# Two of the weight sums of each Strassen pair move from VectorE to GpSimd

## The chip, the cores and the metric

The kernel runs on one core of one Trainium2 chip. The time is the device time of that core in microseconds (us), as the median of several runs. The span in the profile is the time from the first to the last instruction of one profiled execution.

## The reference

Two layers, each a feed-forward block (FFN), a token mixer and a second FFN, on 512 tokens of width 1024, all in float32. The change lies in the FFN, of which there are four in the run:

```python
def swiglu(x, w_in, w_out):
    gate, up = jnp.split(x @ w_in, 2, axis=-1)
    return (jax.nn.silu(gate) * up) @ w_out

# per layer: x is 512 x 1024, D_FF = 2816
hn = rms_norm(h, g_ffn1[l]) * (1.0 + sc1) + sh1
h = h + 0.5 * (1.0 + gt1) * swiglu(hn, w_ffn1_in[l], w_ffn1_out[l])
```

## The kernel before

Activations are held transposed, with the 1024 features in 8 tiles of 128 partitions and the 512 tokens along the free dimension. Every float32 product is made of three matmuls in a reduced format: weights and activations are split into a high part (a rounded copy) and a low part (the rest), and the products high by high, high by low and low by high are added up in PSUM. `split` (L100 to L102) makes the two parts of a tile: a cast on ScalarE (L101) and a subtraction on VectorE (L102).

The hidden width of 2816 is 22 blocks of 128, taken two at a time as 11 pairs, in two groups: pairs 0 to 5 and pairs 6 to 10. After each group comes a stage that multiplies the group's activations by the output weights and adds the result to the residual (L294). The first pairs of an FFN (four in the first FFN, two in the others) are computed in the plain way. All others, 34 over the run, go through `pair_in` (L388 to L429), which computes gate and up of two blocks with a scheme of Strassen's kind. The input width is halved, the tokens are halved, and seven products of a half weight by a half activation take the place of eight. A group's first Strassen pair is called the first pair of a stage in what follows; there are eight such starts.

The weights of a pair are four tiles of 128 by 1024 elements: A(0,0), A(0,1), A(1,0), A(1,1) (512 KB each). `raw` loads one by a DMA that SyncE issues; `plus` adds another one on top of it by an accumulating DMA that GpSimd issues (L334). The tile `S` (named `sum` in the profile, with two buffers sum0 and sum1 used by even and odd pairs) takes three values in turn, and each is split and multiplied:

- the first sum, A(1,0) + A(1,1), made by the two DMAs: product with P1 into `pF`;
- the second sum, with a11 = A(0,0) added (L403): product with P2 into `pD`;
- the third sum, with a12 = A(0,1) added (L413): product with B22 into `pF`.

The other four products are a11 by B11 into `pD`, a12 by B21 into `pG`, S3 = A(0,0) + A(1,0) (two DMAs again, tile `third`) by T3 into `pD`, and A(1,1) by T4 into `pD`. The last one belongs to `rest`, which is put off until the next pair calls `flush`. Since `pD` accumulates over four of the products, it has to be copied out in between: ScalarE copies it after a11's product (L402, tile s1) and after the second sum's product (L407, s2), and the next product onto `pD` waits for that copy. VectorE combines the results (L411, L417, L419, L421, L426) and splits the activations (L386).

Each of the tags wH and wL has four buffers, so splits run up to four products ahead of TensorE; the next cast then waits until TensorE gives a buffer back. Each engine runs its own instructions in order. That order, and the semaphores between the engines, are laid down by the framework when the program is built, from the order of the code, its dependences and its own estimate of when each instruction is ready. So the order in the profile isn't that of the code line by line: in the first pair of a stage, for one, a12's product begins before the second sum's.

GpSimd carries only the issue of DMAs (the accumulating loads, and those of the modulation weights `wada`, L177) and a few fills. The modulation weights are multiplied on VectorE (L163) in the output stages.

## Time and profile before

| | |
|---|---|
| median of 3 runs | 1936.84 us (1936.34 to 1939.99) |
| the profiled execution, its own time | 1942.73 us |
| its span | 1940.6 us |
| TensorE matmuls busy | 1894.4 us (98%) |
| VectorE (DVE) busy | 1400.0 us (72%) |
| ScalarE (ACT) busy | 838.4 us (43%) |
| GpSimd (POOL) busy | 130.8 us (7%) |
| mean granted TensorE clock | 0.990 |

In the views, PE is TensorE, DVE VectorE, ACT ScalarE, POOL GpSimd and SP SyncE. A row of the timeline gives the start in us from the span's start, the duration in us, the engine, the line, the operation, output and inputs by the program's names, and in brackets the idle time of the engine just before it with what ended it. A row of the waits gives who waited for whom: us in total, times, longest. Group rows give the count, the least, median and greatest duration in ns, and the first and last start. Matmuls are pipelined, so their starts say more than their durations.

### The profile page before, as it was taken

How to read it: one execution, taken by the hardware profiler on the slowest of the kernel's cores; microseconds unless marked ns; L12 is line 12 of the kernel's file. 1: busy time of each engine (PE TensorE's matmuls, PEld its weight loads, DVE VectorE, ACT ScalarE, POOL GpSimd, SP SyncE). 2: the span in 40 equal slices, each digit the busy share in tenths (PEclk: the TensorE clock that was granted, in tenths of full speed). 3: DMA queues.
4: the chain of work that ended last, by engine and by line, in shares of the span. 5: the costliest groups of instructions: out<-in, count | busy, mean ns of one | idle time of the engine just before them, and what ended most of it. 6: DMA issues, size and time to landing. Idle time of an engine off the chain costs nothing. (4 is left out here: it accounts for less than half of the span.)

```text
span 1940.6 us, 36814 instructions
## 1 busy us (share of the span) xinstructions
PE 1894.4 (98%) x15392; PEld 1748.4 (90%) x15392; DVE 1400.0 (72%) x2176; ACT 838.4 (43%) x1269; POOL 130.8 (7%) x212
## 2 busy tenths in 40 slices
PE   8999999999999999999999999999999999999999
PEld 7998899797889999899899989988978899998997
DVE  7687687658975787677877776876588578773762
ACT  4443255347422554155345514544562235532551
POOL 0101101000000000110100020010000000010100
PEclk8999999999999999999999999999999999999999
DMA  7767875621222475886746688773222125765742
GB/s 296 250 161 232 258 197 170 211 69 47 54 60 63 133 203 168 279 216 173 227 123 180 171 263 234 184 221 97 88 54 57 51 61 153 205 218 131 197 113 90
DMA packets 104325, 308.44 MB, mean 159 GB/s; under 512 B 23392, under 2 KB 24416, under 8 KB 103136
## 3 DMA queue, kind: packets, MB, share of 16 engines
q1 hardware_dynamic: 75936, 203.34, 32.5%
q0 software_dynamic: 28224, 102.77, 21.5%
q8 instruction: 120, 1.97, 0.4%
q14 instruction: 45, 0.37, 0.1%
HBM read 302.66 MB, written 3.41 MB: 158 GB/s over the span
## 5 line engine op out<-in xcount | busy, mean ns | idle before, releaser
L101 ACT CAST wH<-wraw 128x1024 fp32r<-128x1024 f32 (+2 forms) x292 | 268.9, 922 | 561.7 <-PE ps_mm L91 157.5
L102 DVE TENSOR_TENSOR wL<-wraw,wH 128x1024 fp32r<-128x1024 f32 (+2 forms) x292 | 309.0, 1060 | 123.3 <-ACT wH L101 121.8
L91 PE MATMUL ps_mm<-actL,wH 128*128 128x512 f32 (+1 forms) x744 | 282.5, 380 | 0.0
L90 PE MATMUL ps_mm<-actH,wH 128*128 128x512 f32 (+1 forms) x744 | 282.5, 380 | 0.0
L92 PE MATMUL ps_mm<-actH,wL 128*128 128x512 f32 (+1 forms) x744 | 282.0, 379 | 0.0
L380 PE MATMUL ps_d<-comH,wH 128*128 128x256 f32 x816 | 227.6, 279 | 4.5 <-ACT s L402 3.8
L381 PE MATMUL ps_d<-comL,wH 128*128 128x256 f32 x816 | 226.2, 277 | 0.0
L382 PE MATMUL ps_d<-comH,wL 128*128 128x256 f32 x816 | 226.1, 277 | 0.0
L98 PE MATMUL ps_mm<-hnH,wH 128*128 128x256 f32 x1040 | 213.8, 287 | 5.3 <-ACT hnH L101 2.9
L98 PE MATMUL ps_mm<-hnH,wL 128*128 128x256 f32 x1040 | 213.9, 285 | 0.5 <-DVE wL L102 0.5
L98 PE MATMUL ps_mm<-hnL,wH 128*128 128x256 f32 x1040 | 212.5, 284 | 0.0
L163 DVE SCALAR_TENSOR_TENSOR wada<-wada,crep 128x1024 f32<-128x1024 f32 x140 | 167.8, 1221 | 53.8 <-DMA wada<-in_wadaT 53.6
L102 DVE TENSOR_TENSOR wL<-sum,wH 128x1024 fp32r<-128x1024 f32 x102 | 125.0, 1225 | 70.1 <-ACT wH L101 69.9
L98 PEld LDWEIGHTS ps_mm<-hnH,wH 128*128 128x128 f32 x1040 | 160.8, 191 | 13.6 <-issue 5.5
L101 ACT CAST wH<-sum 128x1024 fp32r<-128x1024 f32 x102 | 107.5, 1054 | 148.0 <-PE ps_d L381 72.1
L98 PEld LDWEIGHTS ps_mm<-hnH,wL 128*128 128x128 f32 x1040 | 161.2, 191 | 6.3 <-issue 4.7
L98 PEld LDWEIGHTS ps_mm<-hnL,wH 128*128 128x128 f32 x1040 | 161.6, 191 | 4.5 <-issue 3.9
L92 PEld LDWEIGHTS ps_mm<-actH,wL 128*128 128x128 f32 x744 | 141.2, 190 | 26.1
L91 PEld LDWEIGHTS ps_mm<-actL,wH 128*128 128x128 f32 x744 | 141.2, 190 | 25.6
L90 PEld LDWEIGHTS ps_mm<-actH,wH 128*128 128x128 f32 x744 | 140.9, 189 | 25.7
L380 PEld LDWEIGHTS ps_d<-comH,wH 128*128 128x128 f32 x816 | 153.9, 189 | 7.1 <-ACT s L402 5.0
L381 PEld LDWEIGHTS ps_d<-comL,wH 128*128 128x128 f32 x816 | 154.1, 189 | 0.0
(401 smaller groups left out, 4245.5 us busy)
## 6 DMA issues: line engine op xcount, KB each, us to landing
wada<-in_wadaT POOLq DMA_DIRECT2D x128, 512.0 KB, 5.0
wraw<-in_wmi SPq DMA_DIRECT2D x40, 512.0 KB
wraw<-in_w2p SPq DMA_DIRECT2D x36, 512.0 KB
wraw<-in_w1p SPq DMA_DIRECT2D x32, 512.0 KB
wraw<-in_w1o SPq DMA_DIRECT2D x32, 384.0 KB
wraw<-in_w2o SPq DMA_DIRECT2D x32, 384.0 KB
wraw<-in_w1i SPq DMA_DIRECT2D x20, 512.0 KB
wraw<-in_w1o SPq DMA_DIRECT2D x32, 320.0 KB
```

What stands on the lines that cost most here:

```text
L90: mm(acc, wH, xH, start=start, stop=False)
L91: mm(acc, wH, xL, start=False, stop=False)
L92: mm(acc, wL, xH, start=False, stop=stop)
L98: mm(acc[:, sl], w[a][:, k], x[b][:, sl], start=start and n == 0 and sl is HALVES[0], stop=stop and n == 2, skip_group_check=True)
L101: nc.scalar.copy(hi, src)
L102: nc.vector.tensor_sub(lo, src, hi.bitcast(F32))
L163: stt(w, w, 1.0, crep, ALU.mult, ALU.mult, accum_out=out_)
L380: mm(pt[:, i], wH, x[k][0], start=start and i + k == 0, stop=False, skip_group_check=True)
L381: mm(pt[:, i], wH, x[k][1], start=False, stop=False, skip_group_check=True)
L382: mm(pt[:, i], wL, x[k][0], start=False, stop=k == 3, skip_group_check=True)
```

## The change

The two additions of weights on the tile `S` are issued on GpSimd in place of VectorE, with the same operands. `tt` is `nc.vector.tensor_tensor`.

```diff
                 prod(pD, hl(a11), B11, True)
                 s1 = half_("s1")
                 nc.scalar.copy(s1, pD)
-                tt(S, S, a11, ALU.add)
+                nc.gpsimd.tensor_tensor(S, S, a11, ALU.add)
                 flush()
                 prod(pD, hl(S), P2, False)
...
                 gate = half_("gate")
                 tt(gate, pG, s1, ALU.add)
                 act(gate, gate, AF.Silu)
-                tt(S, S, a12, ALU.add)
+                nc.gpsimd.tensor_tensor(S, S, a12, ALU.add)
                 S3 = raw(A(0, 0), "third")
                 plus(S3, A(1, 0))
```

## The prediction

> **What bounds the kernel now.** I read the busy table first, then a window over one pair in the middle of a Strassen stage, then the timelines of that pair, and last the list of what TensorE waits for. The window is one pair long (the seven products of `pair_in`).

> ```profile
> core 0: us, PE busy (x) PEld busy (x) DVE busy (x) ACT busy (x) POOL busy (x), PEclk, DMA share, GB/s
> 255.70:274.80 19.10, 19.10 (x170) 19.10 (x169) 15.24 (x16) 11.04 (x15) 1.70 (x2) 1.00 0.76 193
> ```

> TensorE is busy for all 19.10 us, VectorE for 15.24, GpSimd for 1.70. So in the middle of a stage an instruction taken from VectorE returns nothing by itself; what counts is whether the sums still come in time. The group rows of the tile `sum` give the two additions, 34 times each:

> ```profile
> L403 DVE TENSOR_TENSOR sum<-sum,first x34: 1216/1225/1227, 120.1 to 1854.3; 128x1024 f32<-128x1024 f32 x34
> L413 DVE TENSOR_TENSOR sum<-sum,wraw x34: 1215/1218/1226, 123.8 to 1863.0; 128x1024 f32<-128x1024 f32 x34
> ```

> Each takes 1.22 us, 83 us of VectorE time in all. Here they stand in that pair on VectorE (start and duration in us first), each behind the low-part split (L102) that reads the same tile:

> ```profile
> 256.56 1.23 DVE L102 TENSOR_TENSOR wL<-sum,wH 128x1024 fp32r<-128x1024 f32 x1 [0.89 <-ACT wH L101]
> 257.82 1.23 DVE L403 TENSOR_TENSOR sum<-sum,first 128x1024 f32<-128x1024 f32 x1
> ...
> 264.72 1.23 DVE L102 TENSOR_TENSOR wL<-sum,wH 128x1024 fp32r<-128x1024 f32 x1 [0.28 <-ACT wH L101]
> ...
> 266.47 1.22 DVE L413 TENSOR_TENSOR sum<-sum,wraw 128x1024 f32<-128x1024 f32 x1
> ```

> And here is who reads the results on ScalarE:

> ```profile
> 263.63 1.06 ACT L101 CAST wH<-sum 128x1024 fp32r<-128x1024 f32 x1 [1.66 <-PE ps_f L381]
> ...
> 271.83 1.06 ACT L101 CAST wH<-sum 128x1024 fp32r<-128x1024 f32 x1 [1.14 <-PE ps_d L381]
> ...
> 275.51 0.58 ACT L407 COPY s<-ps_d 128x512 f32<-128x512 f32 x1
> ```

> The casts do not wait for the sums. They wait for TensorE to give a weight buffer back. The second sum is ready at 259.05 (257.82 + 1.23) and read at 263.63, so it has 4.58 us to spare; the third is ready at 267.69 and read at 271.83, 4.14 us to spare. The splits have slack too. The matmul group rows of L380 place three products (first and last start behind the durations):

> ```profile
> L380 PE MATMUL ps_f<-hnH,wH x8: 276/276/276, 260.8 to 263.2; 128*128 128x256 f32 x8
> L380 PE MATMUL ps_f<-comH,wH x8: 276/276/276, 263.5 to 265.9; 128*128 128x256 f32 x8
> L380 PE MATMUL ps_d<-hnH,wH x8: 276/278/283, 266.3 to 268.7; 128*128 128x256 f32 x8
> ```

> One product takes 2.7 us (260.8 to 263.5 to 266.3). The split begun at 256.56 ends at 257.79 and feeds the product at 263.5: 5.7 us to spare.

> What is left to gain or lose lies where TensorE does wait, at the first pair of a stage. Of the list of TensorE's waits, two rows touch these lines:

> ```profile
> PE ps_g L382 <- DVE wL L102: 6.1, 5, 1.5
> ...
> PE ps_d L380 <- ACT s L402: 3.8, 3, 1.8
> ```

> Together 9.9 us in 8 waits. That is the ceiling of a gain from this change: 0.5%.

> **The change, part by part.** It removes 34 + 34 additions from VectorE and adds them to GpSimd, with the same operands and the same readers. No transfer is added. What moves is GpSimd's queue: it issues the accumulating loads of `plus`, and in order, so an addition that waits for its operands holds what is queued behind it.

> *Price of an addition on GpSimd.* The trace has no arithmetic on this engine. Its nearest row is a fill:

> ```profile
> L930 POOL MEMSET Sc<- 128x512 f32 x4 | 2.0, 531 | 57.9 <-DVE hn_t L246 57.9
> ```

> That is 0.53 us for 512 elements per partition, 1.06 us for one pass over 1024. An addition reads two tensors and writes one. Lower end: all three overlap as on VectorE, about 1.2 us. Upper end: three passes, 3.2 us. I take two passes, 2.1 us, the middle. [...]

> *Does VectorE go on beside it?* No row shows the two engines reading SBUF together. One end: both run freely. Other end: one after another, a VectorE instruction with two SBUF operands (all splits) waiting until the addition is over. I work out both.

> *Middle of a stage: nothing, in both cases.* The second sum could start at 257.8 and would end at 259.9 (at 261.0 with 3.2 us), before 263.63. The third could start at 265.95, where the split ends, or at 266.5, where it starts now, and would end by 268.6 (269.7), before 271.83. One after another VectorE would be held for at most 15.24 - 2.4 + 4.2 = 17.0 us of 19.1, and its splits have over 5 us to spare. What hides the edit is TensorE's own product time; an addition of over 5.3 us (266.5 to 271.83) would end that.

> *First pair of a stage: here it costs.* Three stage starts (near 690, 830 and 1180 us) have the third sum ahead of the split of a12. The one near 830, on VectorE:

> ```profile
> 830.39 1.23 DVE L403 TENSOR_TENSOR sum<-sum,first 128x1024 f32<-128x1024 f32 x1 [2.97 <-DMA first<-in_w2p]
> 831.54 1.22 DVE L102 TENSOR_TENSOR wL<-first,wH 128x1024 fp32r<-128x1024 f32 x1
> 832.81 1.23 DVE L102 TENSOR_TENSOR wL<-sum,wH 128x1024 fp32r<-128x1024 f32 x1
> 834.07 1.23 DVE L413 TENSOR_TENSOR sum<-sum,wraw 128x1024 f32<-128x1024 f32 x1
> ...
> 835.88 1.22 DVE L102 TENSOR_TENSOR wL<-wraw,wH 128x1024 fp32r<-128x1024 f32 x1
> ```

> On ScalarE:

> ```profile
> 831.73 1.05 ACT L101 CAST wH<-sum 128x1024 fp32r<-128x1024 f32 x1 [0.28 <-DVE sum L403]
> 832.69 1.05 ACT L101 CAST wH<-wraw 128x1024 fp32r<-128x1024 f32 x1
> ...
> 835.88 1.05 ACT L101 CAST wH<-sum 128x1024 fp32r<-128x1024 f32 x1
> 836.83 0.58 ACT L402 COPY s<-ps_d 128x512 f32<-128x512 f32 x1
> ```

> And on TensorE:

> ```profile
> 837.15 0.38 PE L382 MATMUL ps_g<-hnH,wL 128*128 128x256 f32 x1 [1.01 <-DVE wL L102]
> ...
> 838.55 0.28 PE L380 MATMUL ps_d<-comH,wH 128*128 128x256 f32 x1
> ```

> The first thing to see: the copy L402 stands behind the cast of the third sum in ScalarE's queue, and the product at 838.55 writes onto what L402 copies. So a late third sum delays that product. One after another: second sum 830.4 to 832.5; cast of it 832.6 to 833.65; split of a11 832.5 to 833.7, split of the sum to 834.95, split of a12 right behind to 836.1 (1.0 before its old end of 837.1, so the wait of 1.01 goes); third sum 836.1 to 838.2; its cast from 838.3, L402 from 839.25 to 839.85; product at about 839.9. That is 1.35 us later than 838.55. Freely, the third sum runs 835.05 to 837.15, L402 ends at 838.8: 0.3 later. With 3.2 us one after another, both sums add 1.1: 3.55 later. With 1.2 us: 0.5 earlier. Near 1180 the rows have the same order and distances:

> ```profile
> 1180.45 1.23 DVE L403 TENSOR_TENSOR sum<-sum,first 128x1024 f32<-128x1024 f32 x1 [5.47 <-DMA first<-in_w1p]
> ...
> 1184.14 1.22 DVE L413 TENSOR_TENSOR sum<-sum,wraw 128x1024 f32<-128x1024 f32 x1
> ```

> I give the start near 690 the same price; its third sum is the first row here. Two starts (near 1040 and 1647 us) have the third sum behind the split of a12:

> ```profile
> 690.74 1.22 DVE L413 TENSOR_TENSOR sum<-sum,wraw 128x1024 f32<-128x1024 f32 x1
> ...
> 1036.67 1.23 DVE L102 TENSOR_TENSOR wL<-sum,wH 128x1024 fp32r<-128x1024 f32 x1 [1.13 <-ACT wH L101]
> ...
> 1038.41 1.22 DVE L102 TENSOR_TENSOR wL<-wraw,wH 128x1024 fp32r<-128x1024 f32 x1
> ...
> 1040.15 1.22 DVE L413 TENSOR_TENSOR sum<-sum,wraw 128x1024 f32<-128x1024 f32 x1
> ...
> 1647.25 1.22 DVE L413 TENSOR_TENSOR sum<-sum,wraw 128x1024 f32<-128x1024 f32 x1
> ```

> TensorE near 1043, at the first product that needs the copy L402:

> ```profile
> 1043.04 0.39 PE L380 MATMUL ps_d<-comH,wH 128*128 128x256 f32 x1 [1.79 <-ACT s L402]
> ```

> GpSimd can begin the third sum at 1037.95 and end it at 1040.05, 1.3 before 1041.37: freely, about 0.9 of the 1.79 goes. One after another the split of a12 is held until 1040.05 and ends at 1041.25 in place of 1039.63, so a12's product loses 1.6, which is nearly what the later wait gives back. I take +0.25 on average over the two, between -0.9 (freely) and +1.35 (3.2 us). The other three starts show no wait for VectorE, and I cost them at nothing.

> **The sum**, one after another with 2.1 us: 3 x 1.35 + 2 x 0.25 = **+4.6 us**. Freely: 3 x 0.3 - 2 x 0.9 = -0.9. At 3.2 us one after another: 3 x 3.55 + 2 x 1.35 = +13.4. At 1.2 us: 3 x -0.5 - 2 x 0.9 = -3.3. Three of these four corners give a later or an equal time, so I take +4.6. The profiled execution took 1942.73 us (span 1940.6), so its like would take 1947.3; on the median of the runs shown, 1936.84, that is **1941.4 us**.

> **The rivals.**

> 1. *Freely, no stall* (20%): -0.9 us, 1935.9. The sums are longer but off the path, and VectorE does not notice. For it: VectorE idles for 3.9 of 19.1 us in the window. Against: the order on ScalarE, where L402 sits behind the cast.
> 2. *The other side, faster* (15%): VectorE loses two additions just where TensorE waits for its splits, so the 6.1 us row goes, and as the third sum starts earlier part of the 3.8 us row: -5 to -9.9, some 1930. It decides if an addition takes under about 1.5 us with no hold on VectorE, or if the copy L402 comes ahead of the cast in the new order.
> 3. *GpSimd's queue* (10%): the accumulating load of the next pair's first sum goes out between the two additions now:

> ```profile
> 259.27 0.85 POOL L334 DMA_DIRECT2D sum<-in_w1p  x1 [1.74 <-DVE sum L403]
> ...
> DMA to landing us min/median/max: 5.2/7.0/9.6
> ```

> In the code it stands behind the third sum. If it is queued so, it goes out at 268.6 and lands at 275.6 at the median, up to 278.2; its cast (1.05 us), and behind it L407 with 0.58, would end at 277.2 to 279.8. The product which needs L407 is the one ahead of 260.8, at 258.1, and a pair later at 258.1 + 19.1 = 277.2. So nothing to 2.6 us in each of some 26 pairs; with 1 us it is +26, 1963.

> [...]

> **How the numbers follow.** Forecast 55%: +1 to +13 us, of which 36 points lie above 3.9 us. I call over 0.2% (3.9 us) a difference, about what a measurement of this kernel can tell from none. Slower: 0.36 + 0.10 = 0.46. Same: 0.19 of the forecast and rival 1, 0.39. Faster: rival 2, 0.15. The range 1930 to 1954 takes in rival 2's middle and 3.2 us one after another (1950.2), with some room for other starts; it leaves out rival 3 and the tails, under 0.2.

> **What would show it.** Right: L403 and L413 on POOL at about 2.1 us; splits beside them at over 2 us or behind idle time that ends with `POOL sum`; TensorE's list with more for `ps_d L380 <- ACT s L402` and less for `ps_g L382`; the window of a pair still 19.1 us. Wrong: an addition of over 5 us, TensorE waits in the middle of a stage, a late accumulating load in POOL's rows, or a new order on ScalarE. The working assumes that the order on each engine stays as it is; a new one moves each start by up to a few us either way.

## The result, and the profile after

| | before | after |
|---|---|---|
| median (10 runs each, same chip) | 1936.81 us (1933.26 to 1940.78) | 1944.31 us (1938.34 to 1951.3) |
| the profiled execution, its own time | 1942.73 us | 1943.92 us |
| its span | 1940.6 us | 1942.2 us |

The ratio is 1.0043, with a 95% interval of 1.0027 to 1.0058: slower by 0.43%, about 8 us. Measured once more on another occasion, as a control for the experiments, the ratio was 1.0029 (1.0009 to 1.0049), about 6 us. The two profiled executions differ by only 1.6 us in span. That isn't the effect: the ten executions of before spread over 7.5 us and those of after over 13, for which the last section gives the likely reason, and the profiled execution of before is slower than all ten in the table. So totals are compared by medians here, and profiles only stage by stage; a difference from this profile of before comes out rather too small.

The busy table of after:

```profile
PE 1894.8 (98%) x15392; PEld 1749.3 (90%) x15392; DVE 1426.2 (73%) x2108; ACT 837.9 (43%) x1269; POOL 307.8 (16%) x280
```

The first thing to see is VectorE. It gave away 68 additions, 83 us, and its busy time rose, from 1400.0 to 1426.2 us. The group rows say how. First the two additions on GpSimd (count, least, median and greatest ns):

```profile
L403 POOL TENSOR_TENSOR sum<-sum,first x34: 2387/2694/3259, 120.3 to 1856.1; 128x1024 f32<-128x1024 f32 x34
L413 POOL TENSOR_TENSOR sum<-sum,wraw x34: 2386/2777/2802, 125.2 to 1864.1; 128x1024 f32<-128x1024 f32 x34
```

Then the splits of the raw weights on VectorE, from the groups of instructions (busy us, mean ns, idle before), in before:

```profile
L102 DVE TENSOR_TENSOR wL<-wraw,wH 128x1024 fp32r<-128x1024 f32 (+2 forms) x292 | 309.0, 1060 | 123.3 <-ACT wH L101 121.8
L102 DVE TENSOR_TENSOR wL<-first,wH 128x1024 fp32r<-128x1024 f32 x34 | 41.4, 1216 | 0.1
```

and in after:

```profile
L102 DVE TENSOR_TENSOR wL<-wraw,wH 128x1024 fp32r<-128x1024 f32 (+2 forms) x292 | 366.3, 1256 | 140.7 <-ACT wH L101 139.1
L102 DVE TENSOR_TENSOR wL<-first,wH 128x1024 fp32r<-128x1024 f32 x34 | 90.9, 2674 | 16.8 <-ACT wH L101 16.7
```

The splits of a11 went from 1.22 to 2.67 us in the mean: in these two groups alone 57.3 + 49.5 = 107 us came back. The pair in the middle of a stage shows them beside the additions. VectorE in after:

```profile
259.07 4.10 DVE L102 TENSOR_TENSOR wL<-first,wH 128x1024 fp32r<-128x1024 f32 x1 [0.28 <-ACT wH L101]
...
267.28 3.32 DVE L102 TENSOR_TENSOR wL<-wraw,wH 128x1024 fp32r<-128x1024 f32 x1
```

GpSimd in after:

```profile
259.39 2.69 POOL L403 TENSOR_TENSOR sum<-sum,first 128x1024 f32<-128x1024 f32 x1
261.75 1.15 POOL L334 DMA_DIRECT2D sum<-in_w1p  x1
266.73 2.77 POOL L413 TENSOR_TENSOR sum<-sum,wraw 128x1024 f32<-128x1024 f32 x1 [3.84 <-DVE wL L102]
```

A split of 1.22 us takes 4.10 beside one addition and 3.32 beside the other; each ends about 1.1 us after the addition does. Over the run 66 splits beside an addition are held like this. None of the 28 VectorE operations with an input in PSUM that overlap one is (near 690 us, L454 takes 0.68 beside L413). GpSimd is held as well: the third sums that begin while VectorE's L421 (two inputs in SBUF) is at work take 2.77 to 2.80 us, the others 2.39 to 2.42. The casts that read the sums have not moved:

```profile
263.48 1.05 ACT L101 CAST wH<-sum 128x1024 fp32r<-128x1024 f32 x1 [1.72 <-PE ps_f L381]
...
271.68 1.06 ACT L101 CAST wH<-sum 128x1024 fp32r<-128x1024 f32 x1 [1.19 <-PE ps_d L381]
```

And a window one pair long shows TensorE full and VectorE fuller (17.48 us in place of 15.24):

```profile
core 0: us, PE busy (x) PEld busy (x) DVE busy (x) ACT busy (x) POOL busy (x), PEclk, DMA share, GB/s
256.21:275.31 19.10, 19.10 (x171) 19.10 (x170) 17.48 (x14) 11.26 (x16) 6.88 (x4) 1.00 0.75 199
```

So the middle costs nothing. TensorE's products of the Strassen stages come in the same order in both kernels, so their starts can be subtracted one by one. This table does it for each stage, numbered by its first product's start in before: how much later the kernel is after the first two pairs than it was just ahead of the stage. (From the second pair's end to the stage's end the change is 0.00 us in all eight stages, in every kernel of this table.)

| stage start, us | 122 | 227 | 687 | 830 | 1032 | 1180 | 1640 | 1786 | sum |
|---|---|---|---|---|---|---|---|---|---|
| after | +0.45 | -0.72 | +3.35 | -0.42 | -1.63 | +0.93 | +0.64 | -0.03 | +2.6 |
| after, second profile | +0.73 | -0.72 | +3.41 | +1.21 | -0.55 | +2.35 | -1.19 | -0.04 | +5.2 |

One start is alike in both and stands out, that at 687. TensorE's waits in after name it:

```profile
PE ps_g L382 <- DVE wL L102: 6.8, 5, 1.8
...
PE ps_d L380 <- ACT s L407: 2.6, 1, 2.6
...
PE ps_d L382 <- DVE wL L102: 2.0, 2, 1.5
```

The row for L402 (3.8 us before) is gone. The row ps_d L382 is new: near 1044 and 1190 us the split of a11, held by the second sum, is late for its own product. The row for L407 is new too and is a single wait. Its chain, in before, on VectorE, SyncE's queue, GpSimd and ScalarE:

```profile
685.52 1.22 DVE L102 TENSOR_TENSOR comL<-q,comH 128x1024 fp32r<-128x1024 f32 x1
686.77 0.33 SPq L330 DMA_DIRECT2D sum<-in_w2p  x1
690.81 0.86 POOL L334 DMA_DIRECT2D sum<-in_w2p  x1 [20.91 <-DVE silu L454]
697.97 1.05 ACT L101 CAST wH<-sum 128x1024 fp32r<-128x1024 f32 x1 [3.63 <-PE ps_d L381]
```

The same instructions in after, with the addition ahead of them and the copy L407 and TensorE's product behind:

```profile
684.92 3.25 POOL L403 TENSOR_TENSOR sum<-sum,first 128x1024 f32<-128x1024 f32 x1 [12.97 <-DVE wL L102]
685.83 3.42 DVE L102 TENSOR_TENSOR comL<-q,comH 128x1024 fp32r<-128x1024 f32 x1
689.28 0.33 SPq L330 DMA_DIRECT2D sum<-in_w2p  x1
694.11 0.87 POOL L334 DMA_DIRECT2D sum<-in_w2p  x1 [1.10 <-DMA sum<-in_w2p]
701.50 1.04 ACT L101 CAST wH<-sum 128x1024 fp32r<-128x1024 f32 x1 [5.69 <-DMA sum<-in_w2p]
702.46 0.58 ACT L407 COPY s<-ps_d 128x512 f32<-128x512 f32 x1
703.09 0.39 PE L380 MATMUL ps_d<-comH,wH 128*128 128x256 f32 x1 [2.59 <-ACT s L407]
```

Read it downwards. The addition holds VectorE's last split of the combined activations (comL) from 1.22 to 3.42 us. That split reads tile `q`, which lies in the buffer sum1; only when it is over may SyncE load the next pair's sum into sum1, so the load goes out at 689.28 and not at 686.77. The accumulating load follows it, 3.3 us later than before. Before, the cast of that sum waited for TensorE; now it waits for the DMA, and the copy L407, which stands behind the cast in ScalarE's queue, makes TensorE wait 2.59 us.

### The profile page after: what moved, and what is told of

Its sections match the earlier page's. It is cut to its first block, busy times and chain, and to the rows that moved or that the text cites. A ratio compares the mean times of both kernels' runs of the same rounds, so it can differ in the third digit from the quotient of the medians.

```text
span 1942.2 us, 36888 instructions
## 1 busy us (share of the span) xinstructions
PE 1894.8 (98%) x15392; PEld 1749.3 (90%) x15392; DVE 1426.2 (73%) x2108; ACT 837.9 (43%) x1269; POOL 307.8 (16%) x280
## 3 DMA queue, kind: packets, MB, share of 16 engines
HBM read 302.66 MB, written 3.41 MB: 158 GB/s over the span
## 4 chain that ended last, share of the span: by engine, by line
PE 73%; DVE 11%; DMA 9%; ACT 4%; issue 3%; POOL 1%; SPq 0%; ACTq 0%; POOLq 0%; DVEq 0%
PE ps_mm L98 14%; PE ps_mm L91 7%; PE ps_mm L90 7%; PE ps_mm L92 7%; PE ps_d L380 6%; PE ps_d L381 6%; PE ps_d L382 6%; PE ps_f L382 3%; PE ps_f L380 3%; PE ps_f L381 3%; DVE wL L102 2%; DMA wada<-in_wadaT 2%; ACT wH L101 2%; PE ps_g L382 2%; DVE wada L163 1%
## 5 line engine op out<-in xcount | busy, mean ns | idle before, releaser
L101 ACT CAST wH<-wraw 128x1024 fp32r<-128x1024 f32 (+2 forms) x292 | 269.1, 922 | 564.2 <-PE ps_mm L91 160.9
L102 DVE TENSOR_TENSOR wL<-wraw,wH 128x1024 fp32r<-128x1024 f32 (+2 forms) x292 | 366.3, 1256 | 140.7 <-ACT wH L101 139.1
L380 PE MATMUL ps_d<-comH,wH 128*128 128x256 f32 x816 | 227.7, 279 | 3.2 <-ACT s L407 2.6
L381 PE MATMUL ps_d<-comL,wH 128*128 128x256 f32 x816 | 226.5, 278 | 0.0
L382 PE MATMUL ps_d<-comH,wL 128*128 128x256 f32 x816 | 226.5, 278 | 0.0
L101 ACT CAST wH<-sum 128x1024 fp32r<-128x1024 f32 x102 | 107.4, 1053 | 166.5 <-PE ps_d L381 75.0
L102 DVE TENSOR_TENSOR wL<-sum,wH 128x1024 fp32r<-128x1024 f32 x102 | 124.6, 1221 | 60.9 <-ACT wH L101 60.4
L380 PEld LDWEIGHTS ps_d<-comH,wH 128*128 128x128 f32 x816 | 154.3, 189 | 5.4 <-ACT s L407 4.5
L381 PEld LDWEIGHTS ps_d<-comL,wH 128*128 128x128 f32 x816 | 154.4, 189 | 0.0
```

The lines of the kernel that those rows point to most:

```text
L101: nc.scalar.copy(hi, src)
L102: nc.vector.tensor_sub(lo, src, hi.bitcast(F32))
L380: mm(pt[:, i], wH, x[k][0], start=start and i + k == 0, stop=False, skip_group_check=True)
L381: mm(pt[:, i], wH, x[k][1], start=False, stop=False, skip_group_check=True)
L382: mm(pt[:, i], wL, x[k][0], start=False, stop=k == 3, skip_group_check=True)
```

## The experiments

The ratios and intervals are those on record; they are not the quotients of the two medians beside them. The diffs leave out lines that only pass names along.

**Which pairs carry the cost.** Theory: the first pair of each stage alone. Rival: a small loss in every pair. In the first kernel, shown as a diff against after, the eight first pairs keep their sums on VectorE and the other 26 have them on GpSimd (`waiting` is empty in a first pair); the second is the other way round.

```diff
-                X = new_x(p)
+                X, sum_ = new_x(p), nc.gpsimd.tensor_tensor if waiting else tt
...
-                nc.gpsimd.tensor_tensor(S, S, a11, ALU.add)
+                sum_(S, S, a11, ALU.add)
...
-                nc.gpsimd.tensor_tensor(S, S, a12, ALU.add)
+                sum_(S, S, a12, ALU.add)
```

> The two sums stay on VectorE in the first pair of each stage (8 pairs) and go to GpSimd in the other 26. Theory (the cost lies at the first pairs, the middle of a stage is free although VectorE's splits are held there): the time of before, ratio 0.999 to 1.001, TensorE's waits as before. Rival A (held splits and a busier GpSimd queue cost in the middle): the +0.43% stays, 1.003 to 1.005. Rival B (the difference is clock drops that fall by chance): something between, 1.001 to 1.003.

Measured: 1938.28 us beside 1937.46 of before, ratio 0.9999 (0.9984 to 1.0014). The second kernel has `tt if waiting else nc.gpsimd.tensor_tensor`:

> The reverse: GpSimd makes the two sums in the first pair of each stage only (16 additions), VectorE makes the other 52. Theory: the whole cost, ratio 1.003 to 1.006 (+6 to +11 us). Rival A: the time of before, 0.999 to 1.001. Rival B: between.

Measured: 1941.21 us, ratio 1.0022 (1.0008 to 1.0035). Its waits, in the Strassen products:

```profile
PE ps_g L382 <- DVE wL L102: 5.7, 4, 1.8
...
PE ps_d L380 <- ACT s L407: 2.5, 2, 2.3
```

So 52 additions in the middle are free, and 16 at the first pairs cost. The cost is below the 1.003 that the theory expected, and in the range of rival B (clock drops that fall by chance). The record lists a mean granted clock for each execution, and here it is 0.9915 in the mean beside 0.9907 of before; 0.0008 of 1940 us is about 1.6 us, so by this estimate the 4.5 us that it costs in the mean would be about 6 at an equal clock. With the sums of the first pairs on GpSimd the L407 wait is there; the first of the two kernels has no such row.

**Which of the two sums.** Only the second sum (L403) on GpSimd, as a diff against after:

```diff
-                nc.gpsimd.tensor_tensor(S, S, a12, ALU.add)
+                tt(S, S, a12, ALU.add)
```

> Only the second sum goes to GpSimd, in all 34 pairs. Theory: a second sum that ends some 1.5 us later delays everything behind it at a start, and the load order near 700 us is that of the changed kernel: about half to three quarters of the cost, ratio 1.002 to 1.004. Rival (the third sum alone matters, as it stands ahead of the copy L402): 1.000 to 1.001.

Measured: 1947.19 us, ratio 1.0041 (1.0026 to 1.0056), as much as the whole change. TensorE at the start near 687:

```profile
702.30 0.58 PE L380 MATMUL ps_d<-comH,wH 128*128 128x256 f32 x1 [4.28 <-ACT s L407]
```

Then only the third sum (L413) on GpSimd:

```diff
-                nc.gpsimd.tensor_tensor(S, S, a11, ALU.add)
+                tt(S, S, a11, ALU.add)
```

> Only the third sum goes to GpSimd, in all 34 pairs. Theory as in the prediction (a late third sum holds the copy L402 at two or three starts, about 1 us each, and the accumulating load near 700 us is not late): 1.000 to 1.002. Rival (the third sum alone matters): 1.003 to 1.005.

Measured: 1939.97 us, ratio 1.0015 (1.0002 to 1.0029), with no L407 wait and

```profile
PE ps_g L382 <- DVE wL L102: 7.4, 3, 3.6
```

(In this kernel TensorE's order changed at one start, near 128 us; the three waits of this row lie elsewhere, near 834, 1040 and 1641.) The second sum looks like the dearer one, though the two intervals still touch.

**How long an addition the middle bears.** The kernel with the first pairs on VectorE, each sum in the middle followed by a second addition of zero on GpSimd, which leaves the value as it is (in the diff, `add_and_add_zero` stands for a lambda with the two calls, on L392, so L392 is its line in the profile):

```diff
-                X, sum_ = new_x(p), nc.gpsimd.tensor_tensor if waiting else tt
+                X, sum_ = new_x(p), add_and_add_zero if waiting else tt
```

> As the kernel whose first pairs stay on VectorE, but in the other 26 pairs GpSimd makes each sum and then adds a zero to it, so each sum costs two additions, 5.4 us. The build lays down another order on the engines. Theory (the middle is free only while the third sum ends within some 5 us and VectorE, held during additions, keeps under the 19.1 us of a pair): it ends here: the second sum is over 1 us late, the third 0.5 us, VectorE is held up to 10.8 us of a pair on top of 12.8: 1 to 5 us more in each of 26 pairs, ratio 1.013 to 1.065. Rival (GpSimd's work in the middle is off the path whatever it takes): 0.999 to 1.002.

Measured: 1993.43 us, ratio 1.028 (1.0245 to 1.0316). GpSimd in a middle pair and TensorE's wait:

```profile
272.54 2.79 POOL L392 TENSOR_TENSOR sum<-sum,wraw 128x1024 f32<-128x1024 f32 x1 [2.42 <-DVE wL L102]
275.41 3.27 POOL L392 TENSOR_TENSOR sum<-sum,zero 128x1024 f32<-128x1024 f32 x1
```

```profile
PE ps_d L380 <- ACT s L407: 40.6, 26, 2.0
```

ScalarE, behind that pair of additions:

```profile
278.71 1.06 ACT L101 CAST wH<-sum 128x1024 fp32r<-128x1024 f32 x1 [3.07 <-POOL sum L392]
...
281.00 0.62 ACT L385 CAST actH<-gate 128x512 fp32r<-128x512 f32 x1 [1.23 <-DVE gate L426]
```

The pair of additions takes 6.1 us here, and TensorE waits in each of the 26 middle pairs. The cast of the third sum waits for it now, which agrees with the prediction's limit: over about 5.3 us the cover is gone. The wait for L407, which stands two operations behind the cast at 281.00 on ScalarE, comes by VectorE, though: its L426 was late, after VectorE had been held beside both additions. So 40.6 is the price of late sums and held splits together. The order on the engines is that of the first kernel but for one place near 142 us.

**The hold at the start near 687.** After, with the second sum of the first pair in first-group stages made to wait until VectorE's last comL split is over:

```diff
-                X = new_x(p)
+                X, first_ = new_x(p), not waiting and not xs.get(12)
...
-                nc.gpsimd.tensor_tensor(S, S, a11, ALU.add)
+                sum2 = nc.gpsimd.tensor_tensor(S, S, a11, ALU.add); first_ and tc.add_manual_dep(sum2.ins, sums['split'].ins.name, ORDER, reason='behind the last split')
```

> The changed kernel, but at the four starts where VectorE still splits the combined activations the second sum on GpSimd waits until the last of these splits is done, so it can no longer hold it. The order on TensorE, VectorE and GpSimd stays that of the changed kernel. Theory (near 690 us GpSimd's addition holds that split for 2.2 us, the split frees the buffer of the next pair's first sum, so its load, its accumulating load, its cast and the copy L407 behind the cast come 3 us late, and a drop of the granted clock follows): the wait of TensorE for L407 goes, and with it about 4 us: ratio 1.001 to 1.0025. Rival (a late second sum is what costs, and here it ends later still): 1.004 to 1.006.

Measured: 1946.15 us, ratio 1.0039 (1.0018 to 1.006). The comL split is no longer held (1.22 us), the addition starts behind it, and the chain is gone: that start stands at -0.31 us in place of +3.35. But the total did not follow. TensorE's waits and a split at the same start:

```profile
PE ps_g L382 <- DVE wL L102: 9.7, 6, 2.4
...
PE ps_d L380 <- ACT s L407: 0.2, 1, 0.2
```

```profile
689.39 3.05 DVE L102 TENSOR_TENSOR wL<-wraw,wH 128x1024 fp32r<-128x1024 f32 x1
```

The chain through the buffer is shown as cause of the L407 wait. It isn't shown as the cause of the 8 us: without it the waits for splits grew, from 6.8 to 9.7 us, and this split of a12 is held by the third sum as before. Some of it may be chance: the start near 830, which this edit does not touch, is 2.42 us later than in before, and the mean granted clock of this kernel's executions is 0.9898 beside 0.9908 of before.

**The third sum behind a12's split.** First in the kernel before, all on VectorE, to see what the place in the queue is worth by itself (`first_` is true in a stage's first pair, `behind_` is VectorE's split of a12):

```diff
-                tt(S, S, a12, ALU.add)
+                with (tc.issue_after(behind_.ins) if first_ else nullcontext()): tt(S, S, a12, ALU.add)
```

> The kernel before, with both sums on VectorE; at a stage's first pair the third sum is queued behind the split of a12 (six places where the two change places on VectorE, all else in the order of before). Theory (TensorE waits 1.0 to 1.5 us for the split of a12 at five starts because the third sum stands ahead of it): some 2 to 4 us less wait, ratio 0.998 to 1.000, at the limit of what 5 rounds show; TensorE's row ps_g L382 <- DVE wL falls from 6.1 to under 3.5 us. Rival (the copy L402 behind the third sum's cast takes it all back): 1.000, with the row ps_d L380 <- ACT s L402 longer.

Measured: 1937.47 us beside 1938.41, ratio 0.9994 (0.9974 to 1.0014): ps_g waits fall to 2.4 us, L402 waits rise to 4.2, and no gain shows that is clear of the noise; the interval leaves room for one of up to 5 us, so theory and rival are not told apart. Then on GpSimd, together with the edit before:

```diff
-                nc.gpsimd.tensor_tensor(S, S, a12, ALU.add)
+                sum3 = nc.gpsimd.tensor_tensor(S, S, a12, ALU.add); first3_ and tc.add_manual_dep(sum3.ins, behind_.ins.name, ORDER, reason='behind the split of a12')
```

> The kernel after, with the second sum of the first pair of group-0 stages behind VectorE's last comL split (as in the experiment before), and with the third sum of every first pair behind VectorE's split of a12. So neither of these two splits can be held by the GpSimd sum that stands beside it. Theory (the hold of VectorE's splits at the first pairs is what costs): the ps_g waits fall from the 9.7 us of the run with only the second sum held back to under 6, no L407 wait comes back, ratio 1.000 to 1.003. Rival (the sums are simply late, whatever they hold): a third sum that begins later makes its cast and the copy L402 behind it later; the L402 row comes back with 4 us or more in the list of TensorE's waits, and the ratio stays at 1.004 or above.

Measured: 1961.75 us, ratio 1.0125 (1.0097 to 1.0153). TensorE's waits:

```profile
PE ps_d L380 <- ACT s L402: 15.7, 6, 3.4
...
PE ps_g L382 <- DVE wL L102: 1.5, 2, 0.8
```

and the start near 830, on GpSimd, ScalarE and TensorE:

```profile
840.14 3.28 POOL L413 TENSOR_TENSOR sum<-sum,wraw 128x1024 f32<-128x1024 f32 x1 [4.22 <-DVE wL L102]
843.45 1.04 ACT L101 CAST wH<-sum 128x1024 fp32r<-128x1024 f32 x1 [4.04 <-POOL sum L413]
844.40 0.58 ACT L402 COPY s<-ps_d 128x512 f32<-128x512 f32 x1
845.03 0.38 PE L380 MATMUL ps_d<-comH,wH 128*128 128x256 f32 x1 [2.83 <-ACT s L402]
```

The first half of the theory held: the ps_g waits are the hold, and without it they fall from 9.7 to 1.5 us. The total went to the rival: the third sum is then late, its cast is late, and the copy behind it in ScalarE's queue makes TensorE wait, six times over the run. GpSimd's addition costs in either place; ahead of the split is the cheaper one.

After itself, run beside it:

> The kernel after once more, on the same chip as the run with both sums held back. Every theory: 1.003 to 1.006. Its profile tells which of the first profile's waits belong to the kernel and which to one execution: the L407 wait near 703 us and the clock drop behind it should be there again, the ps_g waits again at 5 to 8 us.

Measured: 1943.73 us beside 1937.4, ratio 1.0029 (1.0009 to 1.0049); its waits of 2.8 us for L407 and 7.8 us in the ps_g row are those of the first profile (2.6 and 6.8).

**Shorter holds.** After, with each addition in two of 512 columns, so that a split could come in between:

```diff
-                nc.gpsimd.tensor_tensor(S, S, a11, ALU.add)
+                [nc.gpsimd.tensor_tensor(S[:, h], S[:, h], a11[:, h], ALU.add) for h in (slice(0, 4), slice(4, 8))]
```

(and the same for a12).

> The changed kernel with each addition on GpSimd made in two halves of 512 columns. The build lays down another order on the engines. If GpSimd holds a VectorE split for a whole instruction, the longest split falls from 4.1 us to about 1.2 + 1.4 = 2.6 us. Theory: the cost falls to half, ratio 1.000 to 1.0035. Rival (the price of the addition, not the hold, makes the sums late): 1.004 to 1.007.

Measured: 1963.28 us, ratio 1.0107 (1.0069 to 1.0145). Two halves cost more than one whole, 2 x 1.58 us at the median against 2.69, and no split came in between: the longest split took 4.37 us, against 4.16 in after and the 2.6 expected. A miss: the holds did not become shorter, so it says nothing for shorter holds. The order of the instructions on VectorE, ScalarE and GpSimd, and of the Strassen products on TensorE, is that of after, so a new order isn't the reason; the dearer additions are what is left, which is not shown by itself.

## Why the prediction was right, and where its steps were not

*Nothing in the middle of a stage: right, and for its reason.* 0.00 us in all eight stages. The casts read the sums as late as they did, and the limit of 5.3 us agrees with the kernel of doubled additions.

*The price, 2.1 us: too low.* 2.4 us at the least, 2.69 and 2.78 at the median beside held splits, up to 3.26. The longest, 3.26, is just past the upper end of 3.2, three passes.

*One after another: right.* No row of before shows the two engines together, so this was the author's estimate. The splits of 4.10 and 3.32 us in after show it; rival 1 falls with them. Of the 73 splits that overlap an addition in after, each with two inputs in SBUF, 66 were held; of the 28 operations with an input in PSUM, none. Having begun first did not keep a split from being held: the one at 259.07 had begun 0.32 us ahead of the addition.

*The cost lies at the first pairs: right* (0.9999 without them). *Its path: wrong.* The step that failed is the one that has a12's split right behind the second sum's, the third sum from 836.1 and the product at about 839.9. On two queues both become free to start when the split of the second sum is over, and the prediction let a12's split go first, without a row for it; at the starts near 1040 and 1647 it had let the third sum go first. In after the third sum is first at every start, and holds a12's split at all but the last one. GpSimd, VectorE and ScalarE in after, at the start near 830:

```profile
838.51 2.40 POOL L413 TENSOR_TENSOR sum<-sum,wraw 128x1024 f32<-128x1024 f32 x1 [2.42 <-DVE wL L102]
839.01 2.99 DVE L102 TENSOR_TENSOR wL<-wraw,wH 128x1024 fp32r<-128x1024 f32 x1
841.03 1.04 ACT L101 CAST wH<-sum 128x1024 fp32r<-128x1024 f32 x1 [1.30 <-PE ps_d L381]
```

The cast of the third sum waits for TensorE, not for the sum; L402 is in time, and what is late is a12's split, in the ps_g row. So the prediction's signs for the two rows were both wrong: ps_g rose from 6.1 to 6.8 and 7.8, and L402 went from 3.8 to nothing. The kernel with both sums held back has the order that the prediction had reckoned with near 830, and there its path is real and dearer than it said: 15.7 us in six waits.

*The starts: read in part.* In before the third sum stands ahead of a12's split at six starts and not at three; those near 122, 227 and 1786 were put at nothing, and near 227 a wait of 0.8 us for L402 went away (-0.72 in both profiles). A new order on ScalarE, which the prediction had named as a sign of being wrong, came too: at the starts near 687, 1032 and 1640 the cast of the second sum and L168 changed places. No kernel here has that order with the sums on VectorE, so what it costs by itself is open.

*"No transfer is added": true, and beside the point.* A transfer's start moved. The prediction followed each late sum to its readers, and did not ask which buffer a held split keeps; the load into sum1, the one chain that repeats in both profiles (+3.4 us), was found that way.

*Rival 2, faster:* the L402 wait did go, as it would have it, but the ps_g waits stayed, because VectorE was held; and putting the third sum behind a12's split on VectorE alone gave no gain clear of the noise (0.9994).

*Rival 3:* the chain accumulating load, cast, L407, TensorE is what happened, but at one start and not in the middle, and not through GpSimd's queue: in the middle the load goes out between the additions, at 261.75, and in time. It priced 26 pairs where one was hit.

*Size: in part luck.* Forecast +4.6 us, measured about +8 and +6. Of the sum, the start near 687 was put at 1.35 and gave 3.4, by another chain: 2.6 of the wait and about 1.7 of a clock drop behind it, less a ps_g wait of 1.0 that went. The two near 830 and 1180 were put at 1.35 each and gave -0.4 and +0.9 in one profile, +1.2 and +2.4 in the other; the two near 1032 and 1640, put at 0.25 each, gave -1.6 and +0.6, and -0.6 and -1.2. The path through L402 that carried the forecast gave nothing, and the waits that came in its place happened to add up to the same side and a like size. One reading of the sum was wrong as well: of its four corners two are later and two earlier (-0.9 and -3.3), not three later or equal. The sum over the starts is 2.6 and 5.2 us in two profiles. The prediction had no term for the clock of the last section, which turns a wait into a longer one in some executions (near 704 us of after, 2.6 us into an estimated 4.3). In the second measurement the mean granted clock is 0.9899 beside 0.9909 of before; 0.0010 of 1940 us is an estimate of 2 us out of 5.9 in the mean, which leaves about 4 for the waits themselves. How these divide between the rows stays open: one profile of before and two of after are too few.

## What to carry to other kernels

The work moved to GpSimd was not taken from VectorE here, whose splits beside it read two operands from SBUF and were held (those of a11 from 1.22 to 2.67 us in the mean): count their hold, and follow what a held instruction keeps, its buffer too, and not its result alone. An operation that changes queue also changes what it stands behind: where it and a neighbour become ready together and one holds the other, as here, work out both orders. Slack in the steady part of a loop says nothing about the first pass, and here sums of 2.7 us were free in 26 pairs and cost 6 to 8 us at eight starts.

## What the runs showed of the hardware, not expected

```profile
core 0: us, PE busy (x) PEld busy (x) DVE busy (x) ACT busy (x) POOL busy (x), PEclk, DMA share, GB/s
700.90:704.31 3.41, 1.22 (x10) 1.23 (x11) 1.73 (x2) 2.48 (x3) 1.17 (x2) 1.00 0.55 223
704.31:707.72 3.41, 3.41 (x18) 3.41 (x18) 3.41 (x2) 0.94 (x2) 2.92 (x2) 0.50 1.04 166
707.72:711.13 3.41, 3.41 (x32) 3.41 (x31) 3.03 (x4) 1.70 (x3) 0.00 (x0) 1.00 1.02 251
```

In the first, TensorE is busy for 1.22 of 3.41 us (36%); in the next it has half its clock and does 18 matmuls in place of 32. So the wait of 2.6 us cost an estimated 1.7 more here, half of the next stretch. The profiles of before and after were cut into such stretches, from 60 us on. Of the 8 at the full clock with matmuls busy for less than half of the 3.41 us, 7 were followed by a stretch at half clock; of the 1075 others at the full clock, 2 (matmuls busy for 51 and 57%). One and the same stall was followed by the full clock in one profile and by half of it in another. After, first profile:

```profile
1192.40:1195.81 3.41, 1.64 (x14) 1.45 (x13) 3.41 (x3) 1.53 (x2) 0.83 (x1) 1.00 0.19 35
1195.81:1199.22 3.41, 3.41 (x32) 3.41 (x31) 0.77 (x1) 0.69 (x1) 0.00 (x0) 1.00 0.89 291
```

After, second profile:

```profile
1192.70:1196.11 3.41, 1.63 (x14) 1.43 (x13) 3.41 (x3) 1.53 (x2) 1.25 (x1) 1.00 0.21 61
1196.11:1199.52 3.41, 3.41 (x18) 3.41 (x17) 1.20 (x2) 0.00 (x0) 0.00 (x0) 0.50 0.80 271
```

Between 60 and 1940 us, the profile of before has 23.9 us at half clock, those of after 27.3 and 41.0. With half of each lost, that is an estimated 12, 14 and 20 us: a difference between two runs of one kernel as large as the change itself, and likely the reason for most of the spread. The executions without a profile bear it out: of the 69 of before that were run beside the experiments, the ten with a mean granted clock of 0.988 or less took 1942.0 us in the mean, the fourteen with 0.993 or more 1932.2.
